# First projections of the last tile pair as single tiles; diagonals and gated scalings on ScalarE; a first low part on VectorE

## The chip, the core and the metric

The kernel runs on one core of one Trainium2 chip. The time is the device time of one launch in microseconds. A product is one matmul instruction of TensorE together with its weight load. PE is TensorE, PEld its weight loads, DVE VectorE, ACT ScalarE, POOL GpSimd, SP the engine that issues the transfers.

## What is computed

Two layers of a backbone over 512 latent tokens and 256 context tokens, width 1024, in fp32. Cut to what matters here:

```python
for l in range(DEPTH):
    hc = layer_norm(xc) * (1.0 + mod_c[1]) + mod_c[0]
    hl = layer_norm(xl) * (1.0 + mod_l[:, 1]) + mod_l[:, 0]
    pc, pl = hc @ w_in[l], hl @ w_in[l]      # group A: conv, gates, two scans
    ...                                      # group B: spatial gating, C: Fourier mixing
    y = jnp.concatenate([rms_norm(y_a, g_mix[:D_A]), rms_norm(y_b, ...), rms_norm(y_c, ...)], -1)
    xl = layer_norm(DEEPNORM_ALPHA * xl + mod_l[:, 2] * (y @ w_out), ln1_g[l], ln1_b[l])
    hl = layer_norm(xl) * (1.0 + mod_l[:, 4]) + mod_l[:, 3]
    xl = layer_norm(DEEPNORM_ALPHA * xl + mod_l[:, 5] * swiglu(hl, w_up[l], w_down[l]), ln2_g[l], ln2_b[l])
    ...                                      # context likewise, except in the last layer
```

## The kernel before

**Tiles and precision.** The 768 tokens are six tiles of 128: tiles 0 and 1 are context, 2 to 5 latent. A large product is done three times with split operands: each operand has a high part, rounded to fp32r, and a low part, the rest; `mm` (line 198; line 137 is where each product is emitted) issues high x high, high x low and low x high. So an SBUF operand must be cast (ScalarE, `AF.Copy`) and subtracted (`tt`, line 206, on VectorE or GpSimd) before TensorE can read it. Buffers of the split tokens and weights are named `r`, plain fp32 ones `f`, PSUM tiles `mm` and `aux`. With one weight block of 128 columns, a projection of 1024 inputs takes 8 x 3 = 24 products per stretch of tokens.

**Stages.** Per layer: mixing (`mixing`), which ends in the output projection, and channel mixing (`mlp`), which ends in the down projection. Layer 1 does no output work on the context. In mixing the products stand in an order written out by hand (`STEPS`, one letter a step); elsewhere a scheduler orders each engine's instructions by what it simulates, and the code's order has a say.

**The ends.** `ends` closes mixing and channel mixing. For each tile it issues the projection in two halves, the residual on VectorE, the layer norm (VectorE, with a power on GpSimd for the reciprocal root, line 237), and `normal` (line 650, ScalarE), the normalised tile. `modulate` then transposes that tile on TensorE (8 transposes into `aux`), scales it on ScalarE (line 665), casts (line 671) and subtracts. The last two tiles have nothing behind them, so a fill is woven in: the first projections of the next stage, made by `parts`. A piece (j, i) is the 24 products of projection j on chunk i of the tokens; a chunk is two tiles, 256 columns. `cuts` says how many pieces stand ahead of the transposes of tile 4 and how many between those and the transposes of tile 5; the rest follows. There are three ends with a fill, each of three projections: layer 0's mixing (chunks 0-1, 2-3, 4-5), layer 0's channel mixing (the same) and layer 1's mixing (2-3, 4-5). The third projection of a fill takes its weights only when its first piece comes.

**First modulation.** At the start, `first_mod` (line 413) modulates the transposed tokens one block of 128 channels at a time: a multiply on VectorE for the context (256 columns) and one for the latents (512), a cast on ScalarE, and the low part: context on GpSimd, latents on VectorE. It runs over four blocks, then over the other four; `first_proj` follows block by block, context first.

**RMS norms.** `rms` (line 851) norms a gated tile: square with a sum on ScalarE, power on GpSimd, scaling on VectorE (line 859). `rms_rows` (line 965) does it for transposed data: sums by products with a column of ones (`aux<-ones,f`), power on GpSimd, and one diagonal of 128x128 a tile on GpSimd (line 979), which `rms_put` multiplies with ones to spread it (`mm<-f,ones`) and multiplies onto the data (line 991), then casts (line 996). The scaled split of an output weight is lines 1384 (ScalarE) and 1385 (VectorE).

Of the kernel before, what the change touches and what calls it, by code (L numbers as in the profile page):

```python
# [10 lines left out]
F32 = mybir.dt.float32  # L11
F32R = mybir.dt.float32r
AF = mybir.ActivationFunctionType
ALU = mybir.AluOpType
AX = mybir.AxisListType

P = 128
# [7 lines left out]
NT = NC_T + NL_T  # L25
# [138 lines left out]
class Kernel:  # L164
# [248 lines left out]
    def first_mod(self, ks):  # L413
        nc = self.nc
        for k in ks:
            for s, a, b in ((1, 0, NC_T), (0, NC_T, NT)):
                y = self.raw[:, k, a:b, :]
                nc.vector.tensor_scalar(
                    out=y, in0=y, scalar1=self.modT[:, 1, k, s : s + 1], scalar2=self.modT[:, 0, k, s : s + 1], op0=ALU.mult, op1=ALU.add
                )  # L420
                H, L = (x[:, :, k, :] for x in self.XT(a, b))
                nc.scalar.activation(H, y, AF.Copy)
                self.tt(nc.vector if s == 0 else nc.gpsimd, L, y, H.bitcast(F32), ALU.subtract)

    def first_proj(self, u, ps, ks):
        w = tuple(b.r.rearrange("p (k n) -> p k n", n=P) for b in (u.high, u.low))
# [301 lines left out]
    def parts(self, names, chunks, early):  # L728

        us, ps = self.use_all(names[:early]), []  # L730

        def piece(j, i):
            if j == len(us):
                us.append(self.use(names[j]))
            if i == 0:
                ps.append(self.psum_big())
            a, b = chunks[i]
            w = tuple(x.r.rearrange("p (k n) -> p k n", n=P) for x in (us[j].high, us[j].low))
            for k in range(KC):
                self.mm(ps[j][:, 256 + a * P : 256 + b * P], tuple(x[:, k, :] for x in w), self.rhs_tok(a, b, k), k == 0, k == KC - 1)  # L740
            if i == len(chunks) - 1:
                self.drop(us[j])

        order = [(j, i) for i in range(len(chunks)) for j in range(early)]
        n = len(order) - early
        order = order[:n] + [(j, i) for i in range(len(chunks) - 1) for j in range(early, len(names))] + order[n:]
        order += [(j, len(chunks) - 1) for j in range(early, len(names))]
        return [lambda j=j, i=i: piece(j, i) for j, i in order], ps

    def ln_rows(self, l, which, last):  # L750
# [100 lines left out]
    def rms(self, y):  # L851

        nc = self.nc
        j = self.buf(256)
        ss = self.small(4)
        nc.scalar.activation(j.f, y, AF.Square, accum_out=ss[:, 0:1])
        j.free()
        self.rstd(ss[:, 1:2], ss[:, 0:1], 1.0 / 256, EPS)
        nc.vector.tensor_scalar(out=y, in0=y, scalar1=ss[:, 1:2], scalar2=None, op0=ALU.mult)

    def put_group(self, y, ti, k):

# [102 lines left out]
    def rms_rows(self, tiles, sq, width):  # L965

        nc = self.nc
        n_t = len(tiles)
        ssum = self.psum_aux()
        for n, ti in enumerate(tiles):  # L970
            for i, b in enumerate(sq):
                self.pe.matmul(ssum[:, n : n + 1], b.f[:, ti * P : (ti + 1) * P], self.ones[:, 0:1], start=i == 0, stop=i == len(sq) - 1)
        for b in sq:
            b.free()
        r = self.small(n_t)
        self.rstd(r, ssum[:, 0:n_t], 1.0 / width, EPS)
        dg = self.buf(n_t * P)
        for n in range(n_t):
            nc.gpsimd.tensor_scalar(out=dg.f[:, n * P : (n + 1) * P], in0=self.ident, scalar1=r[:, n : n + 1], scalar2=None, op0=ALU.mult)
        return dg  # L980

    def rms_put(self, tiles, dg, ys, k0):
# [80 lines left out]
    def mixing(self, l, first, gate_rows):  # L1063
        nc, t = self.nc, self.t
        last = l == DEPTH - 1
        tiles = list(range(NC_T, NT)) if last else list(range(NT))
        lo = 256 if last else 0
# [19 lines left out]
        done = {"e": 0, "p": 0}  # L1087
# [6 lines left out]
        m2b, rows = gate_rows or ([], [])  # L1094
# [133 lines left out]
        lnb, lg, lb = self.ln_rows(l, 1, False)  # L1228
# [8 lines left out]
                self.drop(u)  # L1237

        fill, ps = self.parts([f"up{l}.0.0", f"up{l}.0.1", f"up{l}.1.0"], self.chunks(lo), 2)
        self.ends(tiles, project, rows, (lg, lb), 2, fill, (2, 1) if last else (2, 2), done)  # L1240
        for b in m2b + lnb:
            b.free()
        return ps

    def chunks(self, lo):
        return [(a, a + 2) for a in range(lo // P, NT, 2)]

    def residual(self, ti, c, ps, m, eng):

# [22 lines left out]
    def mlp(self, l, first):  # L1272
        nc = self.nc
        last = l == DEPTH - 1
# [7 lines left out]
        for gi, (f0, f1) in enumerate(groups):  # L1282
# [39 lines left out]

            if final:
                fill, ps = self.parts([f"in{l + 1}.a{m}" for m in range(3)], self.chunks(0), 2) if not last else ([], None)
                self.ends(tiles, project, m5, (lg, lb), None if last else 0, fill, (2, 2), done)
                if not last:
                    for b in self.Xb[:NC_T]:
                        b.free()
            else:
                for ti in tiles:  # L1330
                    ps = self.psum_big()
                    for hf in range(2):
                        project(ti, hf, ps[:, hf * 512 : (hf + 1) * 512])
                    self.residual(ti, slice(0, D), ps, m5[1 if ti < NC_T else 0], nc.gpsimd)
                done()
# [237 lines left out]
```

## Time and profile before

| | us |
|---|---|
| median of 3 runs (lowest to highest) | 1482.98 (1482.17 to 1483.97) |
| profiled execution | 1483.5 |
| its span | 1481.4 |
| TensorE busy / weight loads busy | 1403.3 / 1172.6 |
| VectorE / ScalarE / GpSimd busy | 865.3 / 517.4 / 288.2 |

A busy TensorE is one with some product in flight; products overlap, so the pace is read from the starts of a run of products, not from the length of one. In the timeline a row is a run of like instructions that one engine issued, with the idle time ahead of the run and what ended it in brackets.

### The profile page before, as it was taken

The page shows a single profiled execution, that of the slowest core. Times are in us where ns is not written, and L with a number is a line of the kernel's source. Part 1 is how long each engine was busy: PE and PEld are TensorE (multiplying, and loading weights), DVE is VectorE, ACT ScalarE, POOL GpSimd, SP SyncE. Part 2 cuts the span into 40 slices and gives each one's busy share as a digit, 9 for nine tenths or more (in the row PEclk, how much of TensorE's full clock was granted, in tenths as well). Part 3 has the DMA queues.
Part 4 walks back from the last instruction along what each step waited for, and adds up shares of the span by engine and source line. Part 5 has one row for each costly group of instructions (what it writes and reads, how often), then busy time and mean ns, then how long its engine had stood idle before and what let it go on. Part 6 is the DMA issues. An engine that isn't in the chain of part 4 may idle for free.

```text
span 1481.4 us, 18151 instructions
## 1 busy us (share of the span) xinstructions
PE 1403.3 (95%) x7307; PEld 1172.6 (79%) x7307; DVE 865.3 (58%) x1230; ACT 517.4 (35%) x719; POOL 288.2 (19%) x199
## 2 busy tenths in 40 slices
PE   6998898999999999999999998997889999999997
PEld 3777876789888888888888877776678888888885
DVE  6638847779248357536226496579786353362427
ACT  4467435345113203112103155785345232232210
POOL 3302323330030030120030055033330112020201
PEclk9999999999999999999999999998899999999999
DMA  9602455044126053371145015013346143342101
GB/s 325 206 15 89 141 187 183 0 147 154 43 66 204 29 153 117 100 222 63 29 128 185 29 53 147 15 43 100 114 143 198 43 128 114 93 121 78 50 15 57
DMA packets 168419, 160.39 MB, mean 108 GB/s; under 512 B 10344, under 2 KB 126536, under 8 KB 168336
## 3 DMA queue, kind: packets, MB, share of 16 engines
q1 hardware_dynamic: 168224, 158.95, 34.5%
q8 instruction: 57, 0.93, 0.3%
q0 software_dynamic: 112, 0.30, 0.1%
q14 instruction: 26, 0.21, 0.0%
HBM read 157.12 MB, written 2.10 MB: 107 GB/s over the span
## 4 chain that ended last, share of the span: by engine, by line
PE 76%; DVE 12%; ACT 5%; issue 4%; POOL 3%; DMA 1%; SPq 0%; DVEq 0%; ACTq 0%; POOLq 0%
PE mm L137 71%; PE aux L137 5%; POOL smalls L237 2%; DVE f L206 1%; DVE f L684 1%; POOL r L206 1%; DVE r L206 1%; DVE f L1251 1%; DVE f L831 1%; DVE smalls L715 1%; ACT f L665 1%; DVE f L828 1%; DVE r L1385 1%; DVE f L830 1%; ACT f L818 1%
## 5 line engine op out<-in xcount | busy, mean ns | idle before, releaser
L137 PE MATMUL mm<-r,r 128*128 128x512 f32 (+1 forms) x6000 | 1198.0, 361 | 20.2 <-DVE f L1251 6.5
L137 PEld LDWEIGHTS mm<-r,r 128*128 128x128 f32 x6000 | 1009.6, 191 | 198.0 <-DVE f L1251 11.3
L211 ACT ACTIVATE r<-f 128x1024 fp32r<-128x1024 f32 (+2 forms) x210 | 195.0, 953 | 560.2 <-PE mm L137 197.2
L206 DVE TENSOR_TENSOR r<-f,r 128x1024 fp32r<-128x1024 f32 (+2 forms) x232 | 252.1, 1109 | 148.4 <-ACT r L211 123.7
L206 POOL TENSOR_TENSOR f<-f,f 128x1024 f32<-128x1024 f32 x40 | 99.6, 2490 | 636.4 <-DVE f L1251 606.2
L1251 DVE TENSOR_TENSOR f<-mm,f 128x512 f32<-128x512 f32 (+1 forms) x80 | 76.3, 953 | 133.2 <-PE mm L137 132.6
L1266 DVE TENSOR_TENSOR f<-mm,f 128x768 f32<-128x768 f32 (+1 forms) x44 | 36.2, 824 | 169.2 <-PE mm L137 167.5
L206 POOL TENSOR_TENSOR r<-f,r 128x512 fp32r<-128x512 f32 (+2 forms) x52 | 90.0, 1738 | 136.9 <-DVE f L828 45.9
L237 POOL TENSOR_TENSOR smalls<-smalls,neghalf 128x1 f32<-128x1 f32 (+3 forms) x61 | 61.9, 1016 | 246.0 <-DVE smalls L236 245.6
L579 DVE SCALAR_TENSOR_TENSOR f<-f,stc,f 128x512 f32<-128x512 f32 x140 | 102.3, 762 | 5.7 <-DMA f<-in_w_mod_dram 4.5
L206 DVE TENSOR_TENSOR f<-f,f 128x512 f32<-128x512 f32 (+1 forms) x70 | 58.3, 835 | 20.2 <-ACT f L799 18.7
L137 PE MATMUL aux<-r,r 128*128 128x256 f32 x480 | 60.7, 288 | 3.6 <-ACT f L1010 3.6
L137 PEld LDWEIGHTS aux<-r,r 128*128 128x128 f32 x480 | 59.7, 196 | 4.9 <-ACT f L1010 3.8
L665 ACT ACTIVATE f<-aux,modT 128x128 f32<-128x128 f32 x128 | 48.4, 464 | 33.6 <-PE aux L137 31.3
L1265 ACT ACTIVATE f<-mm 128x768 f32<-128x768 f32 (+1 forms) x44 | 30.7, 697 | 77.3 <-PE mm L137 77.2
L137 PE MATMUL aux<-cst,f 128*128 128x128 f32 (+1 forms) x239 | 35.3, 284 | 22.7 <-ACT f L650 12.0
L137 PE MATMUL mm<-f,f 128*128 128x512 f32 (+3 forms) x168 | 52.8, 467 | 4.0 <-ACT f L799 3.0
L650 ACT ACTIVATE f<-f,smalls 128x1024 f32<-128x1024 f32 x19 | 23.6, 1244 | 93.2 <-DVE smalls L649 93.2
L137 PEld LDWEIGHTS aux<-cst,f 128*128 128x128 f32 (+1 forms) x239 | 28.1, 144 | 31.4 <-ACT f L650 14.6
L137 PEld LDWEIGHTS mm<-f,f 128*128 128x128 f32 x168 | 30.9, 193 | 21.0 <-issue 8.6
L783 DVE SCALAR_TENSOR_TENSOR f<-mm,par,f 128x255 f32<-128x255 f32 (+3 forms) x48 | 25.7, 611 | 21.8 <-ACT f L777 21.8
L799 ACT ACTIVATE f<-mm,par 128x768 f32<-128x768 f32 x32 | 28.3, 902 | 15.7 <-PE mm L137 10.7
(128 smaller groups left out, 731.1 us busy)
## 6 DMA issues: line engine op xcount, KB each, us to landing
f<-in_w_mod_dram SPq DMA_DIRECT2D x96, 512.0 KB
f<-in_w_up_dram SPq DMA_DIRECT2D x88, 512.0 KB
f<-in_w_down_dram SPq DMA_DIRECT2D x40, 512.0 KB
f<-in_w_in_dram SPq DMA_DIRECT2D x28, 512.0 KB
f<-in_w_out_dram SPq DMA_DIRECT2D x16, 512.0 KB
f<-in_b_mod_dram SPq DMA_DIRECT2D x6, 512.0 KB
f<-in_x_dram SPq DMA_DIRECT2D x4, 512.0 KB
f<-in_ln_g_dram SPq DMA_DIRECT2D x4, 512.0 KB
```

What stands on the lines that cost most here:

```text
L137: i = f(*args, **kw)
L206: return eng.tensor_tensor(out=out, in0=a, in1=b, op=op)
L211: i = self.nc.scalar.activation(h, src, AF.Copy)
L237: self.nc.gpsimd.tensor_tensor(out=out, in0=v, in1=self.neghalf[:, 0:n], op=ALU.pow)
L579: nc.vector.scalar_tensor_tensor(out=b.f, in0=w, scalar=c, in1=b.f, op0=ALU.mult, op1=ALU.add)
L650: nc.scalar.activation(n.f, x, AF.Identity, bias=nm, scale=r)
L665: nc.scalar.activation(y.f[:, q * P : (q + 1) * P], ps[:, q * P : (q + 1) * P], AF.Identity, bias=self.modT[:, slot, k, s : s + 1], scale= ...
L783: nc.vector.scalar_tensor_tensor(out=o, in0=ps[:, i0 : i0 + o1 - o0], scalar=w(k), in1=o, op0=ALU.mult, op1=ALU.add)
L799: insts.append(nc.scalar.activation(g.f, ps[:, 256:1024], AF.Sigmoid, bias=par[:, col : col + 1]))
L1251: self.nc.vector.tensor_tensor(out=tb.f, in0=ps[:, c], in1=m[:, c], op=ALU.mult)
L1265: nc.scalar.activation(g.f, pg[:, 256 + lo : 1024], AF.Silu)
L1266: nc.vector.tensor_tensor(out=g.f, in0=pu[:, 256 + lo : 1024], in1=g.f, op=ALU.mult)
```

## The change

Four edits. The low part of the context in `first_mod` goes to VectorE. `chunks` makes the last two tiles single chunks, and `parts` puts all pieces of the pair chunks first, those of the early projections ahead of the late one's, and then the singles, tile 4 of all projections before tile 5. The cuts of the ends become (3, 3), but stay (2, 1) in layer 1's mixing. The scaling in `rms` and the diagonals in `rms_rows` become ScalarE instructions with a scale read per partition.

```diff
@@ first_mod
-                self.tt(nc.vector if s == 0 else nc.gpsimd, L, y, H.bitcast(F32), ALU.subtract)
+                self.tt(nc.vector, L, y, H.bitcast(F32), ALU.subtract)
@@ parts
-        order = [(j, i) for i in range(len(chunks)) for j in range(early)]
-        n = len(order) - early
-        order = order[:n] + [(j, i) for i in range(len(chunks) - 1) for j in range(early, len(names))] + order[n:]
-        order += [(j, len(chunks) - 1) for j in range(early, len(names))]
+        pairs = range(len(chunks) - 2)
+        order = [(j, i) for i in pairs for j in range(early)] + [(j, i) for i in pairs for j in range(early, len(names))]
+        order += [(j, i) for i in range(len(chunks) - 2, len(chunks)) for j in range(len(names))]
@@ rms
-        nc.vector.tensor_scalar(out=y, in0=y, scalar1=ss[:, 1:2], scalar2=None, op0=ALU.mult)
+        nc.scalar.activation(y, y, AF.Copy, scale=ss[:, 1:2])
@@ rms_rows
-            nc.gpsimd.tensor_scalar(out=dg.f[:, n * P : (n + 1) * P], in0=self.ident, scalar1=r[:, n : n + 1], scalar2=None, op0=ALU.mult)
+            nc.scalar.activation(dg.f[:, n * P : (n + 1) * P], self.ident, AF.Copy, scale=r[:, n : n + 1])
@@ mixing
-        self.ends(tiles, project, rows, (lg, lb), 2, fill, (2, 1) if last else (2, 2), done)
+        self.ends(tiles, project, rows, (lg, lb), 2, fill, (2, 1) if last else (3, 3), done)
@@ chunks
-        return [(a, a + 2) for a in range(lo // P, NT, 2)]
+        return [(a, a + 2) for a in range(lo // P, NT - 2, 2)] + [(NT - 2, NT - 1), (NT - 1, NT)]
@@ mlp
-                self.ends(tiles, project, m5, (lg, lb), None if last else 0, fill, (2, 2), done)
+                self.ends(tiles, project, m5, (lg, lb), None if last else 0, fill, (3, 3), done)
```

TensorE at the end of layer 0's mixing, around the transposes of tile 5 (`aux<-cst,f`; `mm_2499`, `mm_2524` and the third number are the PSUM tiles of the three projections), before:

```order
L137 MATMUL mm_2524<-r_14336_4096_79,r_36480_1024_1987 128x256
L137 MATMUL mm_2524<-r_8192_4096_77,r_46592_1024_1122 128x256
L137 MATMUL aux_2619<-cst_61,f_30592_1024_2056 128x128 x4
L137 MATMUL aux_2631<-cst_61,f_30592_1024_2056 128x128 x4
L137 MATMUL mm_2660<-r_6144_2048_76,r_35456_1024_1966 128x256
L137 MATMUL mm_2660<-r_12288_2048_78,r_35456_1024_1966 128x256
```

and in the changed kernel:

```order
L137 MATMUL mm_2637<-r_14336_4096_79,r_35456_1024_1966 128x256
L137 MATMUL mm_2637<-r_8192_4096_77,r_33408_1024_2619 128x256
L137 MATMUL aux_2686<-cst_61,f_30592_1024_2056 128x128 x4
L137 MATMUL aux_2697<-cst_61,f_30592_1024_2056 128x128 x4
L137 MATMUL mm_2499<-r_8192_4096_77,r_44416_1024_1113 128x128
L137 MATMUL mm_2499<-r_14336_4096_79,r_44416_1024_1113 128x128
```

The third projection's pair pieces moved ahead of the transposes, and what follows them is single tiles: 144 products of 128 columns where 72 of 256 stood. Between the transposes of tile 4 and of tile 5 there are now 72 products of 256 columns here (48 before); at the end of layer 0's channel mixing 67 (44 before); at the end of layer 1's mixing 24 and 9 singles (24 before).

VectorE in the first half of the first modulation (`r_4096_79` is the low part of the latents, `r_2048_78` that of the context), before:

```order
L418 TENSOR_SCALAR f_6144_155<-f_6144_155,modT 128x256
L418 TENSOR_SCALAR f_6144_155<-f_6144_155,modT 128x512
L418 TENSOR_SCALAR f_6144_155<-f_6144_155,modT 128x256
L418 TENSOR_SCALAR f_6144_155<-f_6144_155,modT 128x512
L206 TENSOR_TENSOR r_4096_79<-f_6144_155,r_4096_77 128x4x128
L418 TENSOR_SCALAR f_6144_155<-f_6144_155,modT 128x256
L206 TENSOR_TENSOR r_4096_79<-f_6144_155,r_4096_77 128x4x128
```

and in the changed kernel:

```order
L418 TENSOR_SCALAR f_6144_155<-f_6144_155,modT 128x256
L418 TENSOR_SCALAR f_6144_155<-f_6144_155,modT 128x512
L418 TENSOR_SCALAR f_6144_155<-f_6144_155,modT 128x256
L206 TENSOR_TENSOR r_2048_78<-f_6144_155,r_2048_76 128x2x128
L418 TENSOR_SCALAR f_6144_155<-f_6144_155,modT 128x512
L206 TENSOR_TENSOR r_4096_79<-f_6144_155,r_4096_77 128x4x128
L206 TENSOR_TENSOR r_2048_78<-f_6144_155,r_2048_76 128x2x128
L206 TENSOR_TENSOR r_4096_79<-f_6144_155,r_4096_77 128x4x128
```

Each block of channels now has a context subtraction in VectorE's queue, eight in all.

VectorE near the end of layer 1's mixing (L1110, after the change L1109, is a gate's multiply; the L206 with three `f` adds up the squares, and its last one is what the sums `aux<-ones,f` on TensorE wait for), before:

```order
L236 TENSOR_SCALAR smalls<-aux 128x4
L1385 SCALAR_TENSOR_TENSOR r_1024_7339<-f_1024_71,par,r_1024_6976 128x1024
L1110 TENSOR_TENSOR f_768_7670<-f_768_7670,f_768_7660 128x512
L1385 SCALAR_TENSOR_TENSOR r_1024_5517<-f_1024_5733,par,r_1024_2851 128x1024
L1385 SCALAR_TENSOR_TENSOR r_1024_7833<-f_1024_7633,par,r_1024_7831 128x1024
L206 TENSOR_TENSOR f_768_1032<-f_768_1032,f_768_7660 128x512
```

and in the changed kernel:

```order
L1384 SCALAR_TENSOR_TENSOR r_1024_453<-f_1024_1116,par,r_1024_7964 128x1024
L1043 TENSOR_TENSOR f_1024_7809<-f_512_7540,smalls 128x4x128
L1109 TENSOR_TENSOR f_768_7204<-f_768_7204,f_768_7095 128x512
L236 TENSOR_SCALAR smalls<-aux 128x4
L206 TENSOR_TENSOR f_768_7175<-f_768_7175,f_768_7095 128x512
```

Two scaled weight splits that stood between the last gate's multiply and the last sum moved behind it.

## Rows read from the trace of the kernel before

**Rows 1.** The page, parts 1 and 4: busy time, chain by engine.

```profile
PE 1403.3 (95%) x7307; PEld 1172.6 (79%) x7307; DVE 865.3 (58%) x1230; ACT 517.4 (35%) x719; POOL 288.2 (19%) x199
...
PE 76%; DVE 12%; ACT 5%; issue 4%; POOL 3%; DMA 1%; SPq 0%; DVEq 0%; ACTq 0%; POOLq 0%
```

**Rows 2.** Line 137's products, two stretches: count, ns min/median/max, first and last start.

```profile
L137 PE MATMUL mm<-r,r x24: 389/389/389, 293.8 to 299.0; 128*128 128x512 f32 x24
...
L137 PE MATMUL mm<-r,r x61: 283/283/283, 337.8 to 345.0; 128*128 128x256 f32 x61
```

**Rows 3.** Line 137's weight loads, four stretches (and the one-column products), columns as above.

```profile
L137 PEld LDWEIGHTS mm<-r,r x60: 192/192/192, 337.9 to 345.0; 128*128 128x128 f32 x60
...
L137 PEld LDWEIGHTS aux<-f,stc x16: 106/110/110, 240.5 to 241.4; 128*32 128x32 f32 x16
...
L137 PEld LDWEIGHTS aux<-ones,f x24: 192/192/295, 202.9 to 205.5; 128*128 128x128 f32 x24
...
L137 PE MATMUL aux<-ones,f x24: 168/250/353, 203.1 to 205.5; 128*128 128x1 f32 x24
...
L137 PEld LDWEIGHTS mm<-f,ones x12: 186/192/192, 238.1 to 239.4; 128*128 128x128 f32 x12
```

**Rows 4.** Timeline of TensorE, end of layer 0's mixing: start, length, run [idle before].

```profile
325.99 5.99 PE L137 MATMUL mm<-r,r 128*128 128x256 f32 x48
333.24 1.09 PE L137 MATMUL aux<-cst,f 128*128 128x128 f32 x8 [1.26 <-ACT f L650]
```

**Rows 5.** Timeline, end of layer 0's channel mixing.

```profile
897.06 1.09 PE L137 MATMUL aux<-cst,f 128*128 128x128 f32 x8 [2.24 <-ACT f L650]
...
904.88 2.34 POOL L206 TENSOR_TENSOR r<-f,r 128x1024 fp32r<-128x1024 f32 x1
904.94 2.29 DVE L649 SCALAR_TENSOR_TENSOR smalls<-smalls 128x1 f32<-128x1 f32 x1 [0.66 <-POOL smalls L237]
...
908.56 1.89 PE L137 MATMUL aux<-cst,f 128*128 128x128 f32 x8 [3.65 <-ACT f L650]
```

**Rows 6.** Timeline, end of layer 1's mixing.

```profile
1112.16 1.09 PE L137 MATMUL aux<-cst,f 128*128 128x128 f32 x8 [3.42 <-ACT f L650]
...
1115.28 12.99 PE L137 MATMUL mm<-r,r 128*128 128x256 f32 x80 [2.03 <-ACT r L671]
```

**Rows 7.** Timeline, last part of layer 1's mixing.

```profile
1032.57 2.58 DVE L1385 SCALAR_TENSOR_TENSOR r<-f,par,r 128x1024 fp32r<-128x1024 f32 x2
...
1035.91 1.84 PE L137 MATMUL aux<-ones,f 128*128 128x1 f32 x8 [10.96 <-DVE f L206]
...
1047.60 2.48 DVE L991 TENSOR_TENSOR f<-mm,f 128x512 f32<-128x512 f32 x4
...
1049.00 11.34 PE L137 MATMUL mm<-r,r 128*128 128x512 f32 x40 [1.42 <-ACT r L996]
...
1057.00 1.15 ACT L1384 ACTIVATE r<-f,par 128x1024 fp32r<-128x1024 f32 x1 [2.55 <-DMA f<-in_w_out_dram]
```

**Rows 8.** Timeline, first modulation, both halves.

```profile
34.80 1.71 POOL L206 TENSOR_TENSOR r<-f,r 128x256 fp32r<-128x256 f32 x2 [8.60 <-ACT r L422]
...
35.83 1.22 DVE L206 TENSOR_TENSOR r<-f,r 128x512 fp32r<-128x512 f32 x1
...
37.30 0.68 DVE L206 TENSOR_TENSOR r<-f,r 128x512 fp32r<-128x512 f32 x1
...
59.57 9.83 PEld L137 LDWEIGHTS mm<-r,r 128*128 128x128 f32 x56 [0.45 <-DVE r L206]
```

**Rows 9.** Lines 979, 859 and 856: durations ns min/median/max, first and last start.

```profile
L979 POOL TENSOR_SCALAR f<-cst,smalls x20: 598/605/1835, 207.6 to 1040.9; 128x128 f32<-128x128 f32 x20
...
L859 DVE TENSOR_SCALAR f<-f,smalls x10: 352/353/355, 218.6 to 1046.7; 128x256 f32<-128x256 f32 x10
...
L856 ACT ACTIVATE f<-f x10: 401/402/422, 217.2 to 1043.3; 128x256 f32<-128x256 f32 x10
```

**Rows 10.** Groups on VectorE by form, 33 to 60 us: busy us, mean ns.

```profile
L418 DVE TENSOR_SCALAR f<-f,modT 128x256 f32<-128x256 f32 x8 | 3.3, 407 | 0.0
```

## The prediction

> **What bounds the kernel now.** First the page: TensorE is busy for 95% of the span, its weight loads for 79%, and 76% of the chain that ended last is TensorE's [rows 1]. So what lengthens TensorE's queue lengthens the kernel, and another engine counts only where TensorE waits for it. The change puts 216 more products into that queue, so the second view is the pace of its products. In a run of 512-column products they start 5.2 us / 23 = 0.226 us apart, in a run of 256-column ones 7.2 / 60 = 0.120 us apart [rows 2]: 256 further columns take 0.106 us, 2.4 columns a nanosecond, and some 14 ns come on top for each product. Third, the weight loads. Each product has one. A load of 128 columns shows 192 ns whether the data are the split halves (r) or plain fp32 (f), one of 32 columns 110 ns [rows 3]: 82 ns for 96 columns, 0.85 ns a column, so 109 ns for 128 columns behind a fixed start. Where the moving side is a single column, nothing but the load can set the pace, and there the loads start 2.6 / 23 = 0.113 us apart [rows 3]. I read this as: a 256-column product (107 ns of streaming) just covers its load, a narrower one does not. Last, the gaps: at the end of each of the three stages that have a fill, TensorE waits for the normalised last tiles [rows 4 to 6]; near the end of layer 1's mixing it waits 11 us for VectorE's sums [rows 7]; in the first modulation it waits for the modulated low parts [rows 8].
>
> **Single tiles: the cost.** Nine first projections (three in each of three fills) treat tiles 4 and 5 as two singles instead of a pair. Before: 9 x 24 = 216 products of 256 columns at 0.120 = 25.9 us. After: 432 of 128 columns, a form that the trace does not hold. Lower bound: the line through the two paces of [rows 2], 0.120 - 0.106 / 2 = 0.067 us, 432 x 0.067 = 28.9, so +3.0 us. Upper bound: the 128-column fp32 product. Its weight loads start 1.3 / 11 = 0.118 us apart and it is issued as two of these records for each product, so 0.236 us; 432 x 0.236 = 102, +76 us. Between them I take the row that isolates the weight load, 0.113 us: 48.8 us, **+22.9 us**. I choose it because r and f loads have the same 192 ns, and because the fp32 run of 128 columns has nearly the same pace per record (0.118) as the run of one column (0.113): the moving width hardly matters there, the load does. With 0.109 it is +21.2, with 0.118 +25.1. No gap hides any of it, since the singles are themselves the fill that TensorE works through with inputs ready.
>
> The Trainium skill speaks against so high a price: in "TensorE: Matmul & The Clock Gate", section "Back-to-back issue gap", a stream of load and matmul pairs sustains about 81 ns per matmul at 128 columns. An estimate by that page of the Trainium skill is 432 x 0.081 = 35.0 us, +9.1 instead of +22.9. No run here shows the form yet; the 0.113 of [rows 3] is slower than that figure.
>
> **The fill's new order: the gain.** Each end issues the last projection, some fill, the transposes of tile 4, more fill, the transposes of tile 5, then the rest.
> End of layer 0's mixing: the cut (3,3) puts 72 instead of 48 pair products ahead of tile 5's transposes after those of tile 4, which now come later themselves. The wait there is 1.26 us [rows 4], against 24 x 0.120 = 2.9 us more cover in each half: gone, -1.3.
> End of layer 0's channel mixing: waits of 2.24 and 3.65 us for the normalised tiles 4 and 5 [rows 5]. Between the projection's last product and tile 5's transposes stand 127 pair products instead of 87: 40 x 0.120 = 4.8 us of cover against 5.9. The wait also has a part that comes from GpSimd: a one-column VectorE instruction lasted 2.29 us beside a weight split on GpSimd [rows 5]. In the new order fewer splits stand there, so I take -5.5.
> End of layer 1's mixing: the cuts stay (2,1); only 9 singles slip in ahead of tile 5's transposes, 1.0 us off a wait of 3.42. The next wait, 2.03 us [rows 6], is for the modulated tile 5. It goes, since 63 singles that need only tile 4 now lie ahead (63 x 0.113 = 7.1 us). Together -3.0.
> Sum **-9.8 us**. Bounds: all waits of [rows 4 to 6], 1.26 + 5.89 + 5.45, give -12.6; if VectorE and ScalarE fall behind as much as cover is won at the second end, -6.
>
> **Diagonals and gated scalings on ScalarE.** GpSimd loses 20 diagonals of 605 ns, VectorE 10 scalings of 353 ns; ScalarE gains 30 instructions, of about 400 ns where 256 wide (its own squares of that width take 402) [rows 9]. In layer 0 TensorE has other products while they run, and ScalarE's last scaling is done, by the rows of its squares, before the gate that it has to read next: nothing. Behind each pair of scalings wait the next squares, since the scalings need GpSimd's power first; were the pairs slower than that, the gate and with it the next sum would come under 1 us late. In layer 1 the order moves more. Ahead of the sum that ends TensorE's 10.96 us wait stand two scaled weight splits of 2.58 us together [rows 7]; now they come after it. Further on, four multiplies that start at 1047.60, behind scalings that wait for GpSimd, release TensorE at 1049.00 [rows 7]; without those scalings VectorE reaches them about two us sooner, but ScalarE, which now holds the scalings, must cast them. Against this: the output weights, whose scaled splits come later now; ScalarE waited for such a load until 1057.00 [rows 7], and TensorE cannot finish a tile without it. Bounds 0 and -6; I take **-2.0 us**, the nearer to nothing because the weights' arrival is not moved by the change.
>
> **First modulation.** Eight context low parts move from GpSimd to VectorE, and VectorE's low parts release TensorE in both halves [rows 8]. By the 256-wide multiply there, 407 ns [rows 10], that is +3.3. Against that, the subtraction that ran beside GpSimd's took 1.22 us, the next, alone, 0.68 [rows 8]; two such, -1.1; and a part of the work behind (small steps of the softplus) moves to the side. **+1.5 us**, bounds 0 (all in VectorE's slack) and +2.5.
>
> **Sum.** +22.9 - 9.8 - 2.0 + 1.5 = +12.6. The profiled execution took 1483.5 us (its span 1481.4); the median of the three runs is 1482.98, 0.5 below. 1483.5 + 12.6 - 0.5 = 1495.6, so **1496 us**, 0.9% slower. Own range of this case: low 21.2 - 12.6 - 6 + 0 = +2.6, high 25.1 - 6 - 0 + 2.5 = +21.6, so 1486 to 1505 us.
>
> **Rivals.**
> First, the loads overlap: the weight load of a single runs while the product before it streams and two are in flight, so singles keep the line of [rows 2]. It is decided by the pace of one single: break-even is (25.9 + 9.8 + 2.0 - 1.5) / 432 = 0.084 us. At 0.067 the singles cost +3.0; the cover of tile 4's singles shrinks to 72 x 0.067 = 4.8 us, so the ends gain only 7. +3.0 - 7 - 2 + 1.5 = -4.5: 1478.5 us, faster. Between 0.067 and 0.091 it is anything from that to no change. For it: 79% busy loads, so they are not dense everywhere, and loads that overlap products in every run. Against: the one-column run, where nothing streams and the loads still stand 0.113 apart.
> By the Trainium skill's 81 ns (the page and section named above) the same sum is +9.1 - 8 - 2 + 1.5 = +0.6: an estimate of 1483.6 us, no change.
> Second, products below 256 columns lose the speed of the split halves and go as plain fp32, 0.236 us each: +76 - 9.8 - 2 + 1.5 = +66, 1549 us. For it: no narrow r product exists in the trace, so nothing excludes it. Against: r products are single records and fp32 ones two, and a record's passes show no reason to change with its width.
> Third, the change does not buy its cover: in each end the normalised tile comes late by as much as the fill grows, since VectorE and ScalarE take weight splits first. Then the ends gain 2 instead of 9.8: +20.4, 1503 us. It stays inside the first case's range.
>
> **How the numbers follow.** Weight load sets the pace (with the third rival in it): 0.62. Loads overlap: 0.22, two thirds of it faster, the rest no change. Fp32 pace: 0.16. A measurement here can tell about 0.2%, 3 us, from no change. Faster by more: 0.15 from the overlap and 0.02 from the lowest corner of the main case, 0.17. Within: 0.06 and 0.04, 0.10. Slower: 0.73. The range takes the main case and nearly all of the overlap case, 1470 to 1507; the fp32 case and some tails, under 0.2, stay out.
>
> **What would show it.** Each step has its place. In the fills after tile 5's transposes: runs of 128-column products, starts 0.11 us apart (main), 0.07 (overlap) or 0.24 (fp32), with weight loads gapless in the first. In the three ends: the waits for the normalised tiles 1.3, 2.2 and 3.7 us gone or below 1, that of 3.4 still over 2. In layer 1's mixing: the wait for VectorE's sums down from 11 to some 8 to 9 us. In the first modulation: no low part on GpSimd, TensorE's last product there 1 to 2 us later. Wrong would be: singles at a pace under 0.084, or ends that win more than 13 us.

## The result, and the profile after

The changed kernel takes 1499.46 us in the median (1498.25 to 1514.0), the kernel before 1482.78 beside it: a ratio of 1.0129, 95% interval 1.0103 to 1.0156. The forecast was 1496 us in a range of 1470 to 1507. The span of the profiled execution is 1498.0 us, 16.6 more than before.

Page, parts 1 and 4, of the changed kernel (for [rows 1]), and from its groups that of the singles, which had no row before (busy us, mean ns):

```profile
PE 1434.8 (96%) x7523; PEld 1207.8 (81%) x7523; DVE 857.5 (57%) x1228; ACT 526.7 (35%) x749; POOL 266.9 (18%) x171
...
PE 79%; DVE 9%; ACT 5%; POOL 3%; issue 2%; DMA 1%; SPq 0%; DVEq 0%; ACTq 0%; POOLq 0%
...
L137 PE MATMUL mm<-r,r 128*128 128x128 f32 x432 | 62.5, 317 | 2.5 <-DVE r L206 2.5
```

TensorE is busy for 31.5 us more and waits less. Where they come from is read by TensorE's milestones: the start of the same product in both traces, after minus before. The difference between two milestones is what the stage between them cost.

| stretch | lag at its start and end, us | cost | forecast |
|---|---|---|---|
| start and first modulation | 0 to -1.7 | -1.7 | +1.5 |
| to the end of layer 0's mixing | -1.7 to -2.1 | -0.4 | 0 |
| that end, with its fill | -2.1 to +4.1 | **+6.2** | 7.6 - 1.3 = +6.3 |
| channel mixing up to its end | +4.1 to +3.9 | -0.2 | 0 |
| that end, with its fill | +3.9 to +17.9 | **+14.0** | 7.6 - 5.5 = +2.1 |
| layer 1's mixing | +17.9 to +12.3 | -5.6 | -2.0 |
| its end, with its fill | +12.3 to +17.2 | **+4.9** | 7.6 - 3.0 = +4.6 |

(7.6 is a third of the 22.9 us forecast for the singles; of the first row's -1.7, 0.4 lies ahead of the first modulation's products.) Two of three fills came out as worked out, one cost 12 us more, and the two smaller terms gained 7 us more than forecast. The timeline of TensorE at the end of layer 0's mixing, the good case, for [rows 4] (a row gives the width of its first product; the second holds 144 singles and 27 wider products behind them):

```profile
335.67 1.04 PE L137 MATMUL aux<-cst,f 128*128 128x128 f32 x8
336.46 19.89 PE L137 MATMUL mm<-r,r 128*128 128x128 f32 x171
```

The wait of 1.26 us is gone. The products and weight loads of the singles, from 337 us on (count, ns min/median/max, first and last start):

```profile
L137 PE MATMUL mm<-r,r x136: 272/276/279, 336.8 to 351.9; 128*128 128x128 f32 x136
...
L137 PEld LDWEIGHTS mm<-r,r x136: 191/192/193, 336.9 to 352.0; 128*128 128x128 f32 x136
```

15.1 us / 135 = 0.112 us a single, its load 192 ns as in [rows 3], and the loads without a gap. Now the bad case, the end of layer 0's channel mixing: the timeline, for [rows 5], then stretches of it (start and end, length, busy us and count of PE, PEld, DVE, ACT and POOL, the granted clock, and two figures on transfers), then its singles.

```profile
900.49 1.09 PE L137 MATMUL aux<-cst,f 128*128 128x128 f32 x8 [0.78 <-ACT f L650]
...
909.45 1.03 PE L137 MATMUL aux<-cst,f 128*128 128x128 f32 x8
910.24 1.65 PE L137 MATMUL mm<-r,r 128*128 128x128 f32 x13
913.73 37.76 PE L137 MATMUL mm<-r,r 128*128 128x128 f32 x179 [1.84 <-DVE r L206]
```

```profile
910.00:914.00 4.00, 2.16 (x20) 2.02 (x19) 2.43 (x1) 1.50 (x3) 2.35 (x1) 1.00 0.47 113
914.00:918.00 4.00, 4.00 (x21) 4.00 (x21) 0.69 (x1) 4.00 (x10) 2.36 (x1) 0.50 1.06 339
...
930.00:942.00 12.00, 12.00 (x58) 12.00 (x58) 6.47 (x12) 2.21 (x3) 5.50 (x4) 0.50 0.30 87
...
945.00:949.00 4.00, 4.00 (x23) 3.47 (x22) 1.03 (x2) 0.00 (x0) 0.00 (x0) 1.00 0.00 0
```

```profile
L137 PE MATMUL mm<-r,r x79: 317/415/421, 913.9 to 930.4; 128*128 128x128 f32 x79
...
L137 PEld LDWEIGHTS mm<-r,r x78: 296/333/338, 913.9 to 930.3; 128*128 128x128 f32 x78
```

The waits of 2.24 and 3.65 us fell to 0.78 and nothing, but after a new wait of 1.84 us, with only singles behind it, the granted clock fell to 0.50 (1.2 GHz) and stayed there for some 31 us, although products and loads are busy without a gap. It was up again by 945 us, behind 24 products of 256 columns that began at 941.5. At the lower level a load lasts 333 ns and a single takes 16.5 / 78 = 0.212 us; 131 singles times 0.100 us more are 13 us. At the end of layer 1's mixing, behind a wait of 1.36 us ahead of the transposes (3.42 in [rows 6]) and one of 0.65 us ahead of the first singles, these kept the full clock; a stretch of it:

```profile
1134.00:1140.00 6.00, 6.00 (x56) 6.00 (x55) 2.05 (x2) 2.96 (x3) 0.00 (x0) 1.00 1.16 319
```

So the theory to be tested: (a) the weight load sets the pace of a single; (b) waits lower the clock, and where nothing but singles stands behind them, these don't bring it back, wider products do. Rivals: a fixed price of an instruction for (a); for (b), a stretch that belongs to the place and has its own length. And the side edits (ScalarE, first modulation) had to be weighed by themselves.

### The profile page after: what moved, and what is told of

Its sections match the earlier page's. It is cut to its first block, busy times and chain, and to the rows that moved or that the text cites. A ratio compares the mean times of both kernels' runs of the same rounds, so it can differ in the third digit from the quotient of the medians.

```text
span 1498.0 us, 18595 instructions
## 1 busy us (share of the span) xinstructions
PE 1434.8 (96%) x7523; PEld 1207.8 (81%) x7523; DVE 857.5 (57%) x1228; ACT 526.7 (35%) x749; POOL 266.9 (18%) x171
## 4 chain that ended last, share of the span: by engine, by line
PE 79%; DVE 9%; ACT 5%; POOL 3%; issue 2%; DMA 1%; SPq 0%; DVEq 0%; ACTq 0%; POOLq 0%
PE mm L137 74%; PE aux L137 5%; POOL smalls L237 2%; POOL r L206 1%; ACT f L665 1%; DVE f L684 1%; DVE f L206 1%; DVE f L1250 1%; DVE r L206 1%; DMA f<-in_w_out_dram 1%; DVE smalls L715 1%; DVE f L827 1%; ACT f L817 1%; ACT f L820 1%; DVE smalls L629 0%
## 5 line engine op out<-in xcount | busy, mean ns | idle before, releaser
L137 PE MATMUL mm<-r,r 128*128 128x512 f32 (+2 forms) x6216 | 1232.0, 361 | 19.9 <-DVE f L1250 8.0
L137 PEld LDWEIGHTS mm<-r,r 128*128 128x128 f32 x6216 | 1044.7, 194 | 195.8 <-DVE f L1250 11.3
L206 DVE TENSOR_TENSOR r<-f,r 128x1024 fp32r<-128x1024 f32 (+2 forms) x240 | 255.1, 1087 | 169.2 <-ACT r L211 141.6
L206 POOL TENSOR_TENSOR f<-f,f 128x1024 f32<-128x1024 f32 x40 | 102.1, 2551 | 641.1 <-DVE f L1250 605.4
L206 POOL TENSOR_TENSOR r<-f,r 128x512 fp32r<-128x512 f32 (+2 forms) x44 | 83.1, 1900 | 145.0 <-ACT r L211 66.3
L579 DVE SCALAR_TENSOR_TENSOR f<-f,stc,f 128x512 f32<-128x512 f32 x140 | 105.6, 778 | 3.9 <-DMA f<-in_w_mod_dram 2.0
L206 DVE TENSOR_TENSOR f<-f,f 128x512 f32<-128x512 f32 (+1 forms) x70 | 54.5, 782 | 19.1 <-ACT f L798 17.0
```

Of the source, the lines that this page charges most:

```text
L137: i = f(*args, **kw)
L206: return eng.tensor_tensor(out=out, in0=a, in1=b, op=op)
L579: nc.vector.scalar_tensor_tensor(out=b.f, in0=w, scalar=c, in1=b.f, op0=ALU.mult, op1=ALU.add)
```

## The experiments

Each diff is against the changed kernel unless said otherwise.

**e1, e11, e10: the side edits.** Into the kernel before: all three (e1), the two on ScalarE (e11), the first modulation's (e10).

```diff
+                self.tt(nc.vector, L, y, H.bitcast(F32), ALU.subtract)
...
+        nc.scalar.activation(y, y, AF.Copy, scale=ss[:, 1:2])
...
+            nc.scalar.activation(dg.f[:, n * P : (n + 1) * P], self.ident, AF.Copy, scale=r[:, n : n + 1])
```

> The kernel before with three of the four edits: the first modulation's low part on VectorE, the diagonals and the gated scalings on ScalarE; the fills stay pairs in the old order. By the prediction's terms (-2.0 and +1.5) it should come out within 1 us of the kernel before, 1482 us. By the two traces, in which TensorE's milestones move forward by 1.5 us in the first modulation, by some 0.6 us more up to the end of layer 0's mixing and by 6.6 us between the start of layer 1's mixing (+17.9) and its output projection (+11.3), it should be 8 to 9 us faster than before, 1474 us.

> The kernel before with the diagonals and the gated scalings on ScalarE alone. By the prediction -2 us, 1480.6 us. If the three side edits together cost 2 us and the first modulation wins 1, this must cost 3: 1485.5 us, with the loss in the last third of layer 1's mixing and at its end.

> The kernel before with the first modulation's edit alone. By the prediction +1.5 us, 1484 us. By the trace of the changed kernel, where the transposes behind it start 1.5 us sooner, and of the three side edits together, 0.9 us sooner: -1 us, 1481.5 us.

Measured: e1 1484.77 us, ratio 1.0014 (1.0006 to 1.0023); e11 1485.54, 1.0015 (1.0006 to 1.0024); e10 1481.92, 0.9995 (0.9986 to 1.0004). The 8 to 9 us that I had read out of the two traces for e1 fell; the side edits don't carry over from one order of the program to another. Alone, the ScalarE edits cost 2.7 us (0.9 to 3.6 by the interval); the first modulation's wins 0.9, which its interval (2.1 won to 0.6 lost) doesn't tell from nothing, though it excludes the forecast 1.5 lost. Timeline of TensorE in layer 1's mixing of e11, for [rows 6, 7], and ahead of it a row of ScalarE and one of VectorE:

```profile
1032.73 1.28 ACT L979 ACTIVATE f<-cst,smalls 128x128 f32<-128x128 f32 x4 [2.91 <-POOL smalls L237]
...
1035.08 1.28 DVE L1385 SCALAR_TENSOR_TENSOR r<-f,par,r 128x1024 fp32r<-128x1024 f32 x1 [2.65 <-ACT r L1384]
...
1037.12 1.84 PE L137 MATMUL aux<-ones,f 128*128 128x1 f32 x8 [12.38 <-DVE f L206]
...
1113.30 1.22 PE L137 MATMUL aux<-cst,f 128*128 128x128 f32 x8 [3.83 <-ACT f L650]
```

The wait for VectorE's sums, which I expected shorter, is 12.38 us for 10.96, that for the normalised tile 3.83 for 3.42. ScalarE now holds the diagonals and waits 2.91 us for GpSimd's power ahead of them. What stands behind them in its queue comes later: the square of line 1111, which the last sum needs, starts at 1034.95 us for 1032.97 before, and VectorE waits 2.65 us for ScalarE's half of a weight split that still stands ahead of that sum. In e10 TensorE's first modulation reads

```profile
35.23 4.27 PE L137 MATMUL mm<-r,r 128*128 128x256 f32 x15 [0.23 <-DVE r L206]
```

where before it waited 0.41 us for a context low part of GpSimd (1.71 us for two in [rows 8]). On VectorE that part takes 0.41 us, and VectorE's own low parts take 0.68 each, where one beside GpSimd's took 1.22 [rows 8]. Not all that the traces gain there is this edit's: between the first product of the first modulation and the transposes behind its last, e10 gains 1.8 us and the changed kernel 1.3, but e2 and e11, without it, also gain 0.6.

**e2: the fills alone** (the changed kernel with those three lines as before).

> The kernel before with the fourth edit alone: singles, new order of the fill, cuts (3,3). If the side edits win 8 to 9 us, the fills must cost the rest of the change's +16.7 and that: +25 us, 1508 us. By the prediction's terms (+22.9 - 9.8) it would be +13, 1496 us.

Measured: 1520.39 us, 1.0242 (1.0221 to 1.0264), 12 us more than I had expected. Its trace lags by 4.7 us after the first fill, by 18.5 after the second (4.1 and 17.9 in the changed kernel); but at the end of layer 1's mixing the clock fell as well, behind a wait of 1.90 us ahead of the first singles; a stretch there:

```profile
1140.00:1162.00 22.00, 22.00 (x97) 21.23 (x97) 9.10 (x12) 5.63 (x7) 0.00 (x0) 0.50 0.55 150
```

That fill cost 21 us here against 4.9 in the changed kernel, with the same products.

**e4: pairs at the end of layer 0's channel mixing**, for which `parts` keeps the old order.

```diff
@@ mlp
-                fill, ps = self.parts([f"in{l + 1}.a{m}" for m in range(3)], self.chunks(0), 2) if not last else ([], None)
-                self.ends(tiles, project, m5, (lg, lb), None if last else 0, fill, (3, 3), done)
+                fill, ps = self.parts([f"in{l + 1}.a{m}" for m in range(3)], [(0, 2), (2, 4), (4, 6)], 2) if not last else ([], None)
+                self.ends(tiles, project, m5, (lg, lb), None if last else 0, fill, (2, 2), done)
```

> The changed kernel, but the fill at the end of layer 0's channel mixing goes back to pairs, the old order and the old cuts. In both theories this takes back 144 x 0.113 - 72 x 0.120 = 7.6 us of singles and gives back some 3.3 us of waits. Theory 'lower clock': the 131 singles that ran there at the lower clock level after the 1.84 us wait cost 0.11 us each on top, 14 us; without them 1499.5 - 7.6 + 3.3 - 14 = 1481 us, and the long stretch at clock 0.50 is gone. Rival 'no clock cost' (the stretch would have come anyway, or its loss is hidden): 1495 us.

Measured: 1497.61 us, 1.0098 (1.0084 to 1.0112): by the time alone, the rival. The trace says otherwise. The long stretch left the channel mixing, which now gained 7.6 us (+4.6 to -3.0), and came up at the end of layer 1's mixing instead, whose singles had kept full clock in the changed kernel; that fill cost 20.7 us. There a wait of 2.62 us stands ahead of them, and a stretch behind it reads

```profile
1112.00:1130.00 18.00, 17.88 (x85) 17.88 (x85) 7.86 (x10) 6.95 (x14) 0.00 (x0) 0.50 0.42 112
```

So the stretch doesn't belong to one place; in these traces it comes where waits meet singles.

**e5: 24 wide products between the wait and the singles.**

```diff
@@ mlp
-                self.ends(tiles, project, m5, (lg, lb), None if last else 0, fill, (3, 3), done)
+                self.ends(tiles, project, m5, (lg, lb), None if last else 0, fill, (3, 2), done)
```

> The changed kernel with one number changed: at the end of layer 0's channel mixing the cuts are (3,2) for (3,3), so that 24 products of 256 columns stand between tile 5's transposes and the singles; the same 144 singles run. Theory 'the wait ahead of the singles drops the clock, and the singles don't bring it back': the 2.9 us of wide products cover the 1.84 us wait, the singles keep full clock, and the time falls by 14 us and 2 of wait, less up to 2.9 of wait for tile 5: 1484 to 1486 us. Rival 'singles there run at the lower level whatever stands ahead of them': 1498 to 1502 us, with the stretch at clock 0.50 still some 30 us long.

Measured: 1487.24 us, 1.0046 (1.0017 to 1.0075). In the trace the clock keeps its upper level through the fill, which costs 0.1 us (+4.3 to +4.4) instead of 14. The wait ahead of the singles is gone; waits of 1.11 and 1.25 us stand ahead of and between tile 5's transposes instead, with the 24 wide products behind them. So e5 alone doesn't tell the wide products from the missing wait. A stretch, and the products in the time for which the changed kernel's are shown above:

```profile
915.00:920.00 5.00, 5.00 (x47) 5.00 (x47) 2.44 (x1) 1.29 (x2) 2.37 (x1) 1.00 1.10 375
```

```profile
L137 PE MATMUL mm<-r,r x147: 273/275/332, 914.0 to 930.4; 128*128 128x128 f32 x139, 128*128 128x256 f32 x8
```

147 starts for 79. Nine of eleven executions took 1484 to 1489 us, two 1504: the step between them is about what one stretch costs. Those two were not profiled.

**e6: a wait made where there was none.** At the end of layer 0's mixing tile 4's singles move ahead of tile 5's transposes.

```diff
@@ mixing
-        self.ends(tiles, project, rows, (lg, lb), 2, fill, (2, 1) if last else (3, 3), done)
+        self.ends(tiles, project, rows, (lg, lb), 2, fill, (2, 1) if last else (3, 6), done)
```

> The changed kernel with the cuts at the end of layer 0's mixing (3,6) for (3,3): tile 4's 72 singles move ahead of tile 5's transposes, and nothing stands between these and tile 5's 72 singles, so TensorE must wait some 2 to 3 us for the modulated tile 5 right ahead of 72 singles, in a fill that ran all its 144 singles at full clock. Theory 'a wait lowers the clock and load-bound singles keep it low': the granted clock falls to 0.50 for those singles, 72 x 0.11 = 8 us, so +10 to +11 us on an execution of the changed kernel, 1509 us. Rival 'the long stretch belongs to the end of layer 0's channel mixing': the wait alone, 1502 us, singles there at clock 1.00.

Measured: 1521.89 us, 1.0254 (1.0230 to 1.0277). The timeline there, then a stretch ahead of the wait and one behind it:

```profile
345.92 1.06 PE L137 MATMUL aux<-cst,f 128*128 128x128 f32 x8
349.00 0.55 PE L137 MATMUL mm<-r,r 128*128 128x128 f32 x3 [2.02 <-ACT r L671]
```

```profile
340.00:346.00 6.00, 6.00 (x56) 6.00 (x56) 4.40 (x5) 2.12 (x2) 0.00 (x0) 1.00 1.07 325
...
356.00:362.00 6.00, 6.00 (x30) 6.00 (x29) 2.88 (x3) 1.90 (x2) 0.00 (x0) 0.50 0.19 67
```

The same kind of single at both levels, the wait between them. This fill cost 16.8 us (+0.2 to +17.0) instead of 6.2: +10.6, as expected. Most of the rest is another long stretch at the end of layer 1's mixing, behind waits of 1.62 and 1.10 us (that fill cost 20 us), which I had not expected. The end of the channel mixing, in the same execution, shows the way back: a wait of 4.13 us, seven singles among nine products, then 46 pair products, the rest of tile 5's transposes, and 135 singles at full clock behind them:

```profile
926.77 1.48 PE L137 MATMUL mm<-r,r 128*128 128x128 f32 x9 [4.13 <-DVE r L206]
...
929.37 7.99 PE L137 MATMUL mm<-r,r 128*128 128x256 f32 x46
```

```profile
931.00:937.00 6.00, 6.00 (x39) 6.00 (x39) 0.00 (x0) 0.00 (x0) 2.11 (x1) 0.71 0.66 180
937.00:945.00 8.00, 8.00 (x74) 8.00 (x74) 2.75 (x2) 4.05 (x10) 5.99 (x4) 1.00 0.01 2
```

**e8: wide products among the singles**, the cuts as in e5. The piece came to stand behind 96 singles, not 72.

```diff
@@ parts (the argument `mid` is set at this end alone)
+        if mid:
+            order.insert(len(order) - len(names), order.pop(len(pairs) * len(names) - 1))
```

> The changed kernel; at the end of layer 0's channel mixing 24 products of 256 columns move from ahead of tile 5's transposes to a place between tile 4's 72 singles and tile 5's 72. The wait ahead of the singles stays. Theory 'the lower level lasts while singles run and ends at wider products': the stretch at clock 0.50 begins at the wait as before, ends at the 24 wide products after some 16 to 20 us instead of 31, and the last 72 singles run at full clock: 6 to 8 us less, 1492 us. Rival 'the stretch has its length whatever runs': 31 us still, 1499 us.

Measured: 1513.22 us, 1.0184 (1.0152 to 1.0216), in two groups: two executions at 1501, the profiled one among them, four at 1513 to 1515. TensorE ahead of the singles, then stretches, with the 24 wide products between 932 and 937 us:

```profile
908.58 0.65 PE L137 MATMUL aux<-cst,f 128*128 128x128 f32 x4 [1.09 <-ACT f L650]
910.49 0.66 PE L137 MATMUL aux<-cst,f 128*128 128x128 f32 x4 [1.25 <-ACT f L665]
910.90 1.65 PE L137 MATMUL mm<-r,r 128*128 128x128 f32 x13
```

```profile
907.00:912.00 5.00, 2.66 (x23) 2.22 (x22) 0.92 (x3) 4.71 (x9) 0.60 (x2) 1.00 0.81 247
912.00:914.00 2.00, 0.55 (x5) 0.41 (x4) 2.00 (x1) 2.00 (x6) 1.82 (x1) 0.62 0.23 52
...
930.00:934.00 4.00, 4.00 (x20) 4.00 (x20) 0.54 (x2) 0.99 (x1) 0.00 (x0) 0.50 0.05 14
934.00:938.00 4.00, 4.00 (x27) 4.00 (x27) 2.69 (x5) 0.00 (x0) 0.00 (x0) 0.71 0.39 117
938.00:942.00 4.00, 4.00 (x38) 4.00 (x38) 1.18 (x3) 0.99 (x1) 2.26 (x3) 1.00 0.21 58
```

The way back is as expected: the level is low through 83 singles, rises during the wide products, and the last 48 singles run at 0.11 us. The fall is not: a mean clock of 0.62 between 912 and 914 us, a quarter of them at 1.00 and the rest at 0.50, puts it at some 912.5, just as the wait of 1.88 us ahead of those 83 singles began. So that wait can't have caused it. What stood ahead are the waits of 1.09 and 1.25 us at tile 5's transposes and 13 singles; in e5 nearly the same two waits, with 24 wide products behind them, were followed by no fall. The gain isn't as expected either: this end cost 12.5 us for 14.0, since those 48 singles win 4.8 us, but tile 5's transposes lost the cover that they had in the changed kernel. The four slower executions weren't profiled. One place speaks against the plain form of the theory. At the end of layer 1's mixing of this kernel, with waits of 1.35 and 1.36 us around the first singles and eight fp32 transposes running as it fell, the clock was back in a few us, with singles alone behind the transposes:

```profile
1128.00:1131.00 3.00, 3.00 (x17) 3.00 (x15) 0.19 (x2) 2.43 (x7) 0.00 (x0) 0.51 0.18 58
1131.00:1140.00 9.00, 9.00 (x82) 9.00 (x82) 2.58 (x3) 2.91 (x6) 0.00 (x0) 1.00 1.07 309
```

**e7: half the weight columns.**

```diff
@@ parts (`o` is the piece's place in its PSUM tile; all other products are as before)
+                if b - a == 1 and 0 < k < KC - 1:
+                    self.mm(o[:64], tuple(x[:, k, :64] for x in w), self.rhs_tok(a, b, k), False, False)
```

> The changed kernel, but 18 of the 24 singles of each piece load only 64 of the 128 weight columns (half of the output channels of these products stay without their sum). The same 432 instructions with the same 128 moving columns. Theory 'the weight load sets the pace of a single': by 0.85 ns a column the load of 64 columns is 55 ns shorter, so the pace at full clock falls from 0.113 to about 0.06 to 0.07 us, and the time by 324 x 0.045 = 14 us, more where the singles run at the lower level: 1475 to 1485 us. Rival 'a fixed price of an instruction or the pass of the narrow moving side': pace 0.113 still, 1499 us.

Measured: 1472.6 us, 0.9935 (0.9923 to 0.9947). The singles behind the wait at the end of the channel mixing (2.18 us here), products and loads:

```profile
L137 PE MATMUL mm<-r,r x70: 220/223/277, 906.8 to 912.0; 128*64 128x128 f32 x52, 128*128 128x128 f32 x18
...
L137 PEld LDWEIGHTS mm<-r,r x70: 134/135/192, 906.9 to 912.0; 128*64 128x64 f32 x52, 128*128 128x128 f32 x18
```

A load of 64 columns lasts 135 ns for 192, 57 less; with 18 full ones at 0.112, the 52 short ones stand (5.2 - 2.0) / 52 = 0.06 us apart. The moving side is the same, so the load set the pace, and the rival with a fixed price falls. No long stretch came either, and the time is 27 us lower: 324 x 0.05 = 16, and most of the rest the lost stretch. The three fills cost 0.9, -3.7 and 1.5 us, for 6.2, 14.0 and 4.9 in the changed kernel. At the end of layer 1's mixing the clock did fall, behind waits of 0.98 and 1.67 us, with transposes running as in e8, and it was back by 1107 us with half-loaded singles alone behind them:

```profile
1104.00:1107.00 3.00, 3.00 (x25) 3.00 (x24) 0.69 (x1) 2.97 (x9) 0.00 (x0) 0.50 0.59 171
1107.00:1112.00 5.00, 5.00 (x70) 5.00 (x69) 1.44 (x2) 1.97 (x3) 0.00 (x0) 0.99 1.05 328
```

**e9, c1, c2: what is left without the long stretch.** e9 has singles only at the end of layer 0's mixing. c1 and c2 have none: the side edits, pairs, and cuts (3,2) at both ends of layer 0 (c1), or (3,3) at the first alone (c2).

```diff
@@ c2, against the kernel before with the side edits
-        self.ends(tiles, project, rows, (lg, lb), 2, fill, (2, 1) if last else (2, 2), done)
+        self.ends(tiles, project, rows, (lg, lb), 2, fill, (2, 1) if last else (3, 3), done)
```

> The changed kernel with singles at the end of layer 0's mixing alone; the ends of layer 0's channel mixing and of layer 1's mixing go back to pairs, the old order and the old cuts. In the trace with pairs at the channel mixing alone, TensorE stood 4.8 us ahead of the kernel before until the end of layer 1's mixing, where the singles met a stretch at the lower clock level. Theory 'what the change costs is narrow products, most of it where the clock is low': without those singles that end costs what it did with the side edits alone, +1.4 to +2, so -3 us against the kernel before, 1479 to 1480 us, in every execution. Rival 'something else in layer 1 costs the time': 1490 us or more.

> The kernel before with the three side edits and, in place of singles, only other cuts: (3,2) for (2,2) at the two ends of layer 0, all fills in pairs. No load-bound products, so no long stretch at clock 0.50. Side edits as measured alone, +2 us; 24 more products of 256 columns ahead of tile 5's transposes take 1.3 us of wait at the end of layer 0's mixing and 2 to 3 of the 5.9 at the end of its channel mixing: 1480 to 1482 us. If the weight splits on VectorE and GpSimd set those waits and not the cover, they stay: 1484 to 1485 us.

> No singles at all: the side edits, and pairs with the cuts (3,3) at the end of layer 0's mixing, the rest as in the kernel before. The cover part of the change without its price. If more cover takes the 1.26 us wait there and nothing else moves: +2 - 1.3, 1483 us. If the weight splits behind it fall as they do with singles at that place, the waits at the end of the channel mixing fall too (2.24 to 1.1, 3.65 to 1.1, in that trace -7 us): 1476 us.

Measured: e9 1482.13 us, 0.9999 (0.9991 to 1.0008), all executions between 1480.8 and 1485.2. c1 1485.23, 1.0017 (1.0007 to 1.0026). c2 **1478.29**, 0.9970 (0.9958 to 0.9982): 0.3% below the kernel before and 1.4% below the changed one. e9 and c1 win at the end of layer 0's channel mixing too (7.6 and 4.1 us), but lose 5.1 and 6.0 at the end of layer 1's mixing, where the wait for the last normalised tile has grown from 3.42 to 7.66 and 7.29 us. That is why e9 missed its 1479 to 1480, and why c1 came to 1485 although the waits at its second end fell. The wait in e9:

```profile
1110.63 1.97 PE L137 MATMUL aux<-cst,f 128*128 128x128 f32 x8 [7.66 <-ACT f L650]
```

The two ends of layer 0 in c2:

```profile
337.87 1.04 PE L137 MATMUL aux<-cst,f 128*128 128x128 f32 x8
340.93 19.31 PE L137 MATMUL mm<-r,r 128*128 128x256 f32 x134 [2.02 <-ACT r L671]
...
899.27 1.62 PE L137 MATMUL aux<-cst,f 128*128 128x128 f32 x8 [1.12 <-ACT f L650]
...
906.07 1.03 PE L137 MATMUL aux<-cst,f 128*128 128x128 f32 x8
```

At the first end the cover wins nothing: the wait moves behind the transposes, where the pairs need the modulated tile 5 (2.02 us; the end costs +1.4). At the second, whose code and cuts are those before, 5.4 us are won, and 7.6 in e9: the waits of 2.24 and 3.65 us are 1.1 or gone. In [rows 5] a weight split on GpSimd stood beside VectorE's work. The multiply that ends tile 5's layer norm on VectorE (line 684) reads, in the kernel before and in c2:

```profile
898.66 3.40 DVE L684 SCALAR_TENSOR_TENSOR f<-f,smalls,f 128x1024 f32<-128x1024 f32 x1
```

```profile
900.08 1.28 DVE L684 SCALAR_TENSOR_TENSOR f<-f,smalls,f 128x1024 f32<-128x1024 f32 x1
```

3.40 us where a split on GpSimd ran beside it until 900.97 (2.94 us from 898.03), 1.28 us with none beside it. The scheduler moved the splits in answer to the changed end of layer 0's mixing; that they make all of the 5 to 7 us was not tested.

## Why the prediction came out nearly right, step by step

**The price of a single** was right: 0.112 us measured for 0.113, e7 shows that the load makes it, and the two fills at full clock cost what it gives, within 0.3 us. The overlap (0.067) and the fp32 pace (0.236) are not what the trace shows. Nor are the 81 ns a matmul at 128 columns that the Trainium skill gives in "TensorE: Matmul & The Clock Gate", section "Back-to-back issue gap": the trace has 112.

**What was missing** is the clock. "With 0.109 it is +21.2, with 0.118 +25.1" took the rows at full clock for the only ones: no term and no rival held singles at 0.212 us. [rows 5] had what led to it, waits of 2 to 4 us in that fill. Behind the second of them, in the kernel before, the clock is at 0.50 for a few us as well, and back with 256-column products:

```profile
910.00:912.00 2.00, 2.00 (x12) 2.00 (x11) 0.00 (x0) 2.00 (x6) 1.95 (x1) 0.50 0.35 62
...
914.00:916.00 2.00, 2.00 (x19) 2.00 (x19) 0.67 (x1) 0.00 (x0) 0.00 (x0) 1.00 0.02 9
```

The change put narrow ones in their place: 13 us.

**The ends.** At the end of layer 0's mixing the 1.26 us went, as forecast, and at layer 1's 3.0 was about right (4.9 - 7.6 = -2.7), though the 3.42 us wait fell to 1.36, not just by one. At the channel mixing 5.1 of the 5.5 came (5.89 us of waits fell to 0.78), but cover need not be the reason: e4 and e9 win as much with pairs and the old cuts there. And the wait of 1.84 us for tile 5's modulation was new. The forecast treated the fill as work with "inputs ready".

**ScalarE** has the wrong sign: alone +2.7 us (e11) for -2.0. In the changed kernel layer 1's mixing gained 5.6 us, its wait for sums is 8.36 us for 10.96, as forecast. But e2, without the ScalarE edits, gains 5.0 there (+18.5 to +13.5), its wait for sums is 8.37, and in its trace too no weight split stands between the last gate's multiply and the last sum. So the step credited ScalarE with an order that came with the new fills; what the edit does alone is e11's wait of 2.91 us in ScalarE's queue. 3.9 us of the gain lie at 977 us, where the kernel before waits 2.71 us for ScalarE (line 799) and has a short stretch at 0.50, and the changed one has neither. Where e11 loses its 2.7 us is only in part placed: from layer 1's sums to the end of the last fill it loses 1.1 us and e1 3.0, while in layer 0's mixing and its end, put at nothing, e11 loses 1.9 and e1 wins 1.1.

**First modulation** has the wrong sign: 0.9 won (e10, within its noise) for 1.5 lost. The step charged VectorE's added instructions and missed that TensorE waited for GpSimd's, twice as long each.

**The sum** was only 4 us off because these offset, and that is luck: +12 at the end with the long stretch against -3 and -4 for the two smaller terms, and -1 of rest. So 1496 came near 1499 with one long stretch; with none in the profiled execution, in e5, the same singles gave 1487.

**Open**: whether the executions that differ by some 15 us (1499 and 1514 in the changed kernel, 1487 and 1504 in e5) differ by one long stretch, as these steps suggest, and why; and the exact condition of a fall. Each trace is one execution. In them long stretches came with waits of 1.62 to 2.62 us ahead of full singles, and in e8 behind two waits of 1.09 and 1.25 us; waits of 0.65 to 1.36 were followed by none (the changed kernel, e5) or a short stretch (the second place in e8). Ahead of half loads 2.18 us was followed by none, 0.98 and 1.67 by a short one. The length of a wait alone doesn't decide it.

## What to carry to other kernels

Price a narrow product by its weight load, and at both clock levels. Where waits may stand ahead of a run of them, leave some wider products between: one number in the cuts was worth 12 us. Before moving an instruction that waits for one engine into another's queue, look at what stands behind it there: in e11 the diagonals brought ScalarE a wait of 2.91 us, and the square behind them came 2 us later. And where a scheduler orders the work, weigh an edit over the whole trace: in c2 it cost 1.4 us where it stood and won 5.4 at an end whose code it left alone, and in e9 a win of 7.6 was lost again at a third end.

## What the hardware showed unexpectedly

TensorE, with products and loads busy without a gap for 28 us (914 to 942 us of the changed kernel), stayed at the lower of its two levels (1.2 GHz) as long as it ran 128-column products behind 128-column loads, and came back with 256- or 512-column products (e6, e8, the changed kernel at 945 us), once each with fp32 transposes and full (e8) or half-loaded (e7) singles. At the upper level the same singles kept it there. By level a single takes 0.112 or 0.212 us, its load 192 or 333 ns.
